# Forgetting attention: one product of 129 columns for two, and a longer read-out at the end of a chunk

## The chip, the cores and the metric

One core of a Trainium2 chip. It has five engines that work side by side, each through its own queue in order: TensorE (PE in the profile, its weight loads PEld), VectorE (DVE), ScalarE (ACT), GpSimd (POOL) and SyncE (SP), which here issues DMAs. TensorE multiplies; its results land in PSUM, the accumulators, eight banks of 512 float32 columns in 128 partitions, from where VectorE and ScalarE read them. Everything else lies in SBUF. The metric is the device time of one execution in microseconds; lower is better. The kernel before takes 1131.02 us, the median of three runs (1130.87 to 1131.43).

## The reference

One decoder layer with two kinds of attention heads beside each other, sequence 2048, width 1024, all float32:

```python
h = rms_norm(x, g_pre) * (1.0 + scale) + shift          # scale, shift, gate from c @ w_ada
qa, ka, va, fa, za, qb, kb, vb, zb = split(h @ w_in)
oa = forgetting_attention(qa, ka, va, fa + b_fgate)      # 8 heads of 64, causal
oa = oa * silu(za)
ob = sliding_window_sink_attention(rope(qb), rope(kb), vb, sinks)   # 8 heads, window 128
y = concatenate([oa, ob * silu(zb)]) @ w_out
return x + gate * rms_norm(y, g_post)

def forgetting_attention(q, k, v, f_logit):              # per head
    cum = cumsum(log_sigmoid(f_logit))
    s = q @ k.T * scale + cum[query] - cum[key]          # -inf above the diagonal
    return softmax(s) @ v
```

The change touches the last line, `softmax(s) @ v`, of the eight forgetting heads.

## The kernel before

float32 values are carried as pairs of float16 numbers, a high and a low part. A product of two such numbers takes three matmuls: high by high, high by low, low by high.

The program goes through stages: normalisation and modulation; the projections; the sliding-window heads, with projections between; the forgetting heads, with the remaining projections and the first of the output products between (some 456 to 977 us); the output projection. In the forgetting stage the order of the work on all engines is written out by hand. A head has four chunks of 512 queries (ci = 0 to 3), and a chunk with index ci has 2 (ci + 1) steps of two key blocks of 128: 20 steps a head (NS), 160 in all. For a step:

- `scores()` (L1414 to L1417) puts the transposed scores of 1024 columns or fewer into one tile `sta` of PSUM (one buffer, two banks);
- `exp32()` (L1421), on ScalarE, takes the exponential into SBUF;
- `high()` (L1425), on ScalarE, makes the high part of the probabilities, `low()` (L1428), on VectorE, the low part, into `pha`;
- `pv()` (L1430 to L1451) multiplies probabilities and values. The probabilities are the stationary operand (a weight load for each matmul), and the values, as they lie in `vt`, are streamed: 129 columns for a key block and a head (VW), of which 0 to 63 are the high part, column 64 is ones (it sums the probabilities, the softmax denominator), 65 to 128 are the low part. For each of up to four query blocks u there are three matmuls: L1438 (65 columns, high by high), L1440 (64 columns, high by low) and L1441 (65 columns, low by high). All add into `poa`, four query blocks of 65 columns, in one bank with a single buffer, over all steps of the chunk.

At the chunk's last step the result is read out: VectorE takes the reciprocal of the four sums (L1445) and multiplies (L1447) into `ona`, which is stored (`o_store`).

The loop over steps (L1749 to L1820) runs, for step s: `exp32` of s; one `tick()`; `low` of s - 1; the first half of the fillers; `high` of s; `scores` of s + 1; a second `tick()`; `pv` of s - 2 (PV_LAG); the second half of the fillers. Fillers are projection matmuls (L361), whose results ScalarE and VectorE take out of PSUM, and matmuls for the row maxima of the next head (L1365), which VectorE reduces (L1368, or with the mask L1370), and at the end of a group of four query blocks turns into rows (L1377 to L1385). `after(n, f)` puts f off to the n-th tick from here. So what `pv` issues directly stands on VectorE ahead of the evacuations of the step's second half; what is put off by one tick stands behind them, in the next step, behind `exp32` of that step on ScalarE and ahead of `low` on VectorE.

Of the kernel before, what the change touches and what calls it, by code (L numbers as in the profile page):

```python
# [10 lines left out]
F32 = mybir.dt.float32  # L11
# [4 lines left out]
AF = mybir.ActivationFunctionType  # L16
ALU = mybir.AluOpType
AX = mybir.AxisListType

P = 128  # L20
# [4 lines left out]
CH = 512  # L25
# [10 lines left out]
XM, XR, VW = 66, 69, 129  # L36
# [7 lines left out]
def hybrid_layer(  # L44
# [17 lines left out]
    V, A, G, PE, SP = nc.vector, nc.scalar, nc.gpsimd, nc.tensor, nc.sync  # L62
# [20 lines left out]
    def sm(n, tag):  # L83
        return small.tile([P, n], F32, tag=tag, name=tag)
# [117 lines left out]
    def after(n, f):  # L202
        late.append([n, f])
# [91 lines left out]
    def o_store(on, pool, ci, rows_, cols_, eng, lag):  # L295
        if ci == 0:
            eng.dma_start(o_d[0][rows_, cols_].rearrange("(u p) c -> p u c", p=P), on)
            return
        u0, u1 = rows_.start // P, rows_.stop // P
        oh = pool.tile([P, u1 - u0, 2, on.shape[-1]], F16, tag="oh", name="oh")  # L300

        def low():
            V.tensor_tensor(oh[:, :, 1], on, oh[:, :, 0], op=ALU.subtract)
            eng.dma_start(o_d[ci][u0:u1, :, :, cols_].rearrange("u n p c -> p (u n) c"),
                          oh[:].rearrange("p u n c -> p (u n) c"))

        after(lag, lambda: A.activation(oh[:, :, 0], on, AF.Copy))
        after(lag + 1, low)
# [174 lines left out]
    start = ExitStack()  # L483
# [298 lines left out]
    def swa_pool(name, bufs, **kw):  # L782
        return swa.enter_context(tc.tile_pool(name=name, bufs=bufs, reuse_waits="tile", **kw))

    op_ = swa_pool("op", 3)
# [146 lines left out]
    class Pair:  # L932
# [65 lines left out]
        def pv(self):  # L998
            j, i = self.j, self.i
            po = ps_pv.tile([P, 4, 64], F32, tag="pv", name="pob")  # L1000
            for e, (i_, k0, nk) in enumerate(self.blocks):
                for h in range(2):
                    for b in range(nk):
                        for n, (pp_, vv) in enumerate(((0, 0), (0, 1), (1, 0))):
                            PE.matmul(po[:, 2 * e + h, :], self.ptt[b + 2 - nk][:, pp_, 2 * e + h, :],  # L1005
                                      vb[:, k0 + b, self.g, 64 * vv:64 * vv + 64],
                                      start=(b == 0 and n == 0), stop=(b == nk - 1 and n == 2))

            def out_():
                on = onp.tile([P, 2, P], F32, tag="on", name="on")  # L1010
                V.tensor_tensor(on[:].rearrange("p e (h d) -> p (e h) d", h=2), po[:],
                                self.rinv[:].unsqueeze(2).broadcast_to([P, 4, 64]), op=ALU.mult)
                o_store(on[:], onp, i // 4, slice((i % 4) * P, (i % 4 + 2) * P), slice((4 + j) * P, (5 + j) * P), G, 1)

            after(1, out_)
# [254 lines left out]
    def fox_pool(name, bufs, **kw):  # L1270
        return fox.enter_context(tc.tile_pool(name=name, bufs=bufs, reuse_waits="tile", **kw))

    ps_st = fox_pool("ps_st", 1, space=PSUM)
    ps_po = fox_pool("ps_po", 1, space=PSUM)
# [4 lines left out]
    op_ = foxl.enter_context(tc.tile_pool(name="opa", bufs=2, reuse_waits="tile"))  # L1279
# [52 lines left out]
    vt, lk, lq = fx["vt"], fx["lk"], fx["lq"]  # L1332
# [63 lines left out]
    class Step:  # L1396
# [33 lines left out]
        def pv(self):  # L1430
            hd, ph = self.hd, self.ph
            if self.first:
                self.po_[0] = ps_po.tile([P, 4, 65], F32, tag="po", name="poa")
            po = self.po_[0]
            for n, (b, u0, o) in enumerate(self.blocks):
                for u in range(u0, 4):
                    pq = slice(o + (u - u0) * P, o + (u - u0 + 1) * P)
                    PE.matmul(po[:, u, :], ph[:, 0, pq], vt[:, b, hd, 0:65],  # L1438
                              start=(self.first and n == 0 and u == 0), stop=False)
                    PE.matmul(po[:, u, 0:64], ph[:, 0, pq], vt[:, b, hd, 65:VW], start=False, stop=False)  # L1440
                    PE.matmul(po[:, u, :], ph[:, 1, pq], vt[:, b, hd, 0:65], start=False,  # L1441
                              stop=(self.last and n == len(self.blocks) - 1))
            if self.last:
                rinv = sm(4, "a_ri")
                V.reciprocal(rinv[:], po[:, :, 64])  # L1445
                on = op_.tile([P, 4, 64], F32, tag="ona", name="ona")
                V.tensor_tensor(on[:], po[:, :, 0:64], rinv[:].unsqueeze(2).broadcast_to([P, 4, 64]), op=ALU.mult)  # L1447
                if hd == 7 and self.ci == 0:
                    for t in range(2):
                        G.tensor_copy(outs[t].o[:, 7 * 64:8 * 64], on[:, t, :])  # L1450
                o_store(on[:], op_, self.ci, slice(0, CH), slice(hd * 64, (hd + 1) * 64), SP, 1 if hd == 7 else 2)  # L1451

        po_ = {}

# [231 lines left out]
    outs = [Out(t) for t in range(NB)]  # L1686
# [26 lines left out]
    with tc.manual_schedule():  # L1713
# [35 lines left out]
        for s, stp_ in enumerate(steps):  # L1749
            hd, r = divmod(s, NS)  # L1750
# [118 lines left out]
```

## Time and profile before

| | before |
|---|---|
| median of three runs | 1131.02 us |
| profiled execution | 1129.92 us, of it span 1128.2 us |
| TensorE busy | 1110.6 us (98%) |
| VectorE busy | 905.6 us (80%) |
| ScalarE busy | 656.8 us (58%) |
| GpSimd busy | 224.6 us (20%) |
| granted TensorE clock | 0.999 |

In the profile's rows `L1438` is a line of the kernel's text. A row of instructions in order of time begins with its start in us from the start of the span and its duration; `[0.29 <-PE poa L1441]` tells how long the engine stood idle before it and what released it. A row of a group ends with busy time, the mean duration in ns, and the idle time before. Ends of matmuls are modelled: a matmul of 65 columns is shown with some 0.19 us, though the next one starts 0.03 us later. What one costs in a stream is therefore read from start to start.

### The profile page before, as it was taken

The numbers are of one execution on the slowest core, as the hardware profiler recorded it, in microseconds if no ns is written. First come the engines' busy times: TensorE is split into PE (matmuls) and PEld (weight loads), VectorE is DVE, ScalarE is ACT, GpSimd is POOL, SyncE is SP. The second block draws the span as 40 slices with busy tenths as digits, with TensorE's granted clock in tenths as the row PEclk, the third lists the DMA queues.
The fourth block names the chain that finished last, engine by engine and source line by source line (L and its number), as shares of the span: only waits on it lengthen the run. The fifth ranks groups of instructions, "written<-read, shape, count | busy, mean of one in ns | idle before, by whom it ended". The sixth has DMA issues, their size and how long they took to land.

```text
span 1128.2 us, 25138 instructions
## 1 busy us (share of the span) xinstructions
PE 1110.6 (98%) x9854; PEld 652.4 (58%) x9854; DVE 905.6 (80%) x1988; ACT 656.8 (58%) x1145; POOL 224.6 (20%) x343
## 2 busy tenths in 40 slices
PE   7899999999999999999999999999999999999997
PEld 2566555676756856556555555655556565544444
DVE  8897488878887468898998989988897997766663
ACT  3974345555555412666766667676666889543332
POOL 3111145545556420010010111001000000100000
PEclk9999999999999999999999999999999999999999
DMA  9854434413333142244223333224311245797632
GB/s 364 280 154 96 81 103 90 93 53 92 83 80 89 39 93 51 65 103 44 58 72 74 86 57 87 51 52 71 72 39 46 76 142 164 153 258 213 193 127 102
DMA packets 124653, 119.77 MB, mean 106 GB/s; under 512 B 66009, under 2 KB 102274, under 8 KB 124534
## 3 DMA queue, kind: packets, MB, share of 16 engines
q1 hardware_dynamic: 113662, 85.66, 28.4%
q0 software_dynamic: 10720, 32.46, 12.6%
q8 instruction: 77, 1.26, 0.6%
q14 instruction: 42, 0.34, 0.1%
q10 hardware_dynamic: 152, 0.04, 0.0%
HBM read 64.43 MB, written 25.18 MB: 79 GB/s over the span
## 4 chain that ended last, share of the span: by engine, by line
PE 83%; DVE 9%; DMA 3%; ACT 3%; issue 2%; SPq 0%; POOL 0%; DVEq 0%; POOLq 0%; ACTq 0%
PE bk L361 32%; PE bk L1650 14%; PE bk L379 7%; PE sta L1414 5%; PE sta L1415 5%; PE bk L1365 5%; PE poa L1440 3%; PE poa L1441 3%; PE poa L1438 3%; PE bk L854 2%; DMA wa<-in_w_ada_dram 2%; PE pss L948 2%; PE pob L1005 1%; PE px L453 1%; DMA xt<-in_x_dram 1%
## 5 line engine op out<-in xcount | busy, mean ns | idle before, releaser
L1421 ACT ACTIVATE p<-sta,lift,scl_qk 128x1024 f32<-128x1024 f32 (+2 forms) x160 | 171.8, 1074 | 128.1 <-PE sta L1415 78.9
L361 PE MATMUL bk<-hT,wh_qk 128*128 128x512 f16 x768 | 196.4, 378 | 0.0
L1428 DVE TENSOR_TENSOR pha<-p,pha 128x1024 f16<-128x1024 f32 (+2 forms) x160 | 168.9, 1056 | 0.2 <-ACT pha L1425 0.2
L1650 PE MATMUL bk<-wohl,oz 128*128 128x512 f16 x744 | 163.2, 379 | 0.0
L1368 DVE TENSOR_REDUCE a_m<-bk 128x1 f32<-128x512 f32 x192 | 130.1, 685 | 37.8 <-PE bk L1365 37.3
L1425 ACT ACTIVATE pha<-p 128x1024 f16<-128x1024 f32 (+2 forms) x160 | 147.8, 924 | 4.9 <-PE poa L1441 0.2
L1650 PEld LDWEIGHTS <-oz 128*128 128x128 f16 x744 | 71.0, 98 | 83.1
L1441 PE MATMUL poa<-vt,pha 128*128 128x65 f16 x1088 | 115.9, 192 | 0.7 <-DVE pha L1428 0.7
L1440 PE MATMUL poa<-vt,pha 128*128 128x64 f16 x1088 | 116.2, 194 | 0.0
L1438 PE MATMUL poa<-vt,pha 128*128 128x65 f16 x1088 | 116.2, 193 | 0.0
L361 PEld LDWEIGHTS <-wh_qk 128*128 128x128 f16 x768 | 71.8, 97 | 73.2 <-issue 1.3
L1414 PE MATMUL sta<-T 128*128 128x512 f16 (+1 forms) x320 | 110.9, 346 | 0.7 <-ACT p L1421 0.7
L1365 PE MATMUL bk<-T 66*128 66x512 f16 (+2 forms) x320 | 110.4, 348 | 0.5 <-DVE a_m L1368 0.2
L1415 PE MATMUL sta<-T 69*128 69x512 f16 (+1 forms) x320 | 109.8, 348 | 0.0
L1438 PEld LDWEIGHTS <-pha 128*128 128x128 f16 x1088 | 101.5, 96 | 14.3 <-issue 0.6
L1440 PEld LDWEIGHTS <-pha 128*128 128x128 f16 x1088 | 100.8, 97 | 11.4
L1441 PEld LDWEIGHTS <-pha 128*128 128x128 f16 x1088 | 100.9, 99 | 0.8 <-DVE pha L1428 0.8
L361 PE MATMUL bk<-hT,wh_za 128*128 128x512 f16 x384 | 100.4, 378 | 0.0
L361 PE MATMUL bk<-hT,wh_zb 128*128 128x512 f16 x384 | 92.1, 379 | 0.0
L379 PE MATMUL bk<-wh_va,hT 128*128 128x256 f16 x768 | 91.9, 273 | 0.0
L361 PE MATMUL bk<-hT,wh_qb 128*128 128x512 f16 x384 | 91.2, 379 | 0.0
L404 POOL DMA_DIRECT2D z_d<-tz x32 | 17.7, 555 | 342.5 <-DVE tz L402 250.9
(463 smaller groups left out, 1956.0 us busy)
## 6 DMA issues: line engine op xcount, KB each, us to landing
hT<-in_x_dram SPq DMA_DIRECT2D x20, 512.0 KB
wa<-in_w_ada_dram SPq DMA_DIRECT2D x16, 512.0 KB
z_d<-tz POOLq DMA_DIRECT2D x32, 256.0 KB, 3.1
T<-z_d SPq DMA_DIRECT2D x16, 512.0 KB
T<-stq SPq DMA_DIRECT2D x60, 128.0 KB
out_dram<-hT SPq DMA_DIRECT2D x15, 512.0 KB
xt<-in_x_dram SPq DMA_DIRECT2D x12, 512.0 KB
qs<-qf SPq DMA_DIRECT2D x80, 64.0 KB
```

The source lines that it names most:

```text
L361: PE.matmul(ps, whl[:, a, k, :], hT[ci][:, b, k, :], start=(k == 0 and n == 0), stop=(k == KT - 1 and n == 2))
L379: PE.matmul(ps[:, (u % 2) * 2 * P:(u % 2 + 1) * 2 * P], hT[ci][:, a, k, u * P:(u + 1) * P], wv[p][:, b, k, :], start=(k == 0 and n == 0), ...
L1365: PE.matmul(mx[:, :w], T[0:XM, 0, i * P:(i + 1) * P], T[0:XM, 2, pc * CH:pc * CH + w], start=True, stop=True)
L1414: PE.matmul(self.st[:, o:o + w], T[:, 3, kb_], T[:, 1, qc], start=True, stop=False)
L1415: PE.matmul(self.st[:, o:o + w], T[0:XR, 2, kb_], T[0:XR, 0, qc], start=False, stop=not diag)
L1421: A.activation(self.p32[:, :self.w], self.st[:, :self.w], AF.Exp, scale=scl[f"qk{self.hd}"][:], bias=lift[:])
L1425: A.activation(self.ph[:, 0, :self.w], self.p32[:, :self.w], AF.Copy)
L1428: V.tensor_tensor(self.ph[:, 1, :self.w], self.p32[:, :self.w], self.ph[:, 0, :self.w], op=ALU.subtract)
L1438: PE.matmul(po[:, u, :], ph[:, 0, pq], vt[:, b, hd, 0:65], start=(self.first and n == 0 and u == 0), stop=False)
L1440: PE.matmul(po[:, u, 0:64], ph[:, 0, pq], vt[:, b, hd, 65:VW], start=False, stop=False)
L1441: PE.matmul(po[:, u, :], ph[:, 1, pq], vt[:, b, hd, 0:65], start=False, stop=(self.last and n == len(self.blocks) - 1))
L1650: PE.matmul(py, self.hl[:, i, k, :], w_slot(8 * j + k)[:, cc], start=(k == 0 and m_ == 0), stop=(k == KT - 1 and m_ == 2))
```

## The change

For the query blocks u = 0, 1, 2 the accumulator has 129 columns in place of 65, so that one matmul streams all of `vt`'s 129 columns past the high probabilities: high by high, the sums, and high by low, in columns of their own. The third matmul (65 columns, low by high) stays as it is. The fourth block keeps its three matmuls, since four times 129 columns don't fit in one bank of 512 (three times 129 and 65 is 452). High by low now lies 65 columns beside the rest and has to be added when the chunk is read out: ScalarE copies those three halves of 64 columns (192 in all) into `ona`, VectorE takes the reciprocals, multiplies the fourth block, adds the three blocks' main halves from PSUM to the copy, and multiplies them. This read-out moves to a function of its own, `out_`, which is put off by one tick.

```diff
             if self.first:
-                self.po_[0] = ps_po.tile([P, 4, 65], F32, tag="po", name="poa")
+                self.po_[0] = ps_po.tile([P, CH], F32, tag="po", name="poa")
...
                     pq = slice(o + (u - u0) * P, o + (u - u0 + 1) * P)
-                    PE.matmul(po[:, u, :], ph[:, 0, pq], vt[:, b, hd, 0:65],
+                    c0, wide = u * VW, VW if u < 3 else 65
+                    PE.matmul(po[:, c0:c0 + wide], ph[:, 0, pq], vt[:, b, hd, 0:wide],
                               start=(self.first and n == 0 and u == 0), stop=False)
-                    PE.matmul(po[:, u, 0:64], ph[:, 0, pq], vt[:, b, hd, 65:VW], start=False, stop=False)
-                    PE.matmul(po[:, u, :], ph[:, 1, pq], vt[:, b, hd, 0:65], start=False,
+                    if u == 3:
+                        PE.matmul(po[:, c0:c0 + 64], ph[:, 0, pq], vt[:, b, hd, 65:VW], start=False, stop=False)
+                    PE.matmul(po[:, c0:c0 + 65], ph[:, 1, pq], vt[:, b, hd, 0:65], start=False,
                               stop=(self.last and n == len(self.blocks) - 1))
             if self.last:
-                rinv = sm(4, "a_ri")
-                V.reciprocal(rinv[:], po[:, :, 64])
-                on = op_.tile([P, 4, 64], F32, tag="ona", name="ona")
-                V.tensor_tensor(on[:], po[:, :, 0:64], rinv[:].unsqueeze(2).broadcast_to([P, 4, 64]), op=ALU.mult)
...
+                after(1, self.out_)
+
+        def out_(self):
+            hd, po = self.hd, self.po_[0]
+            on = op_.tile([P, 4, 64], F32, tag="ona", name="ona")
+            p3 = po[:, 0:3 * VW].rearrange("p (u c) -> p u c", c=VW)
+            A.activation(on[:, 0:3], p3[:, :, 65:VW], AF.Copy)
+            rinv = sm(4, "a_ri")
+            V.reciprocal(rinv[:], po[:, 64:3 * VW + 65:VW])
+            V.tensor_scalar(on[:, 3], po[:, 3 * VW:3 * VW + 64], rinv[:, 3:4], None, op0=ALU.mult)
+            V.tensor_tensor(on[:, 0:3], on[:, 0:3], p3[:, :, 0:64], op=ALU.add)
+            V.tensor_tensor(on[:, 0:3], on[:, 0:3], rinv[:, 0:3].unsqueeze(2).broadcast_to([P, 3, 64]), op=ALU.mult)
...
+            o_store(on[:], op_, self.ci, slice(0, CH), slice(hd * 64, (hd + 1) * 64), SP, 1 if hd == 7 else 2)
```

In the changed text the products are L1439 (129 columns, or 65 for the fourth block), L1442 (64) and L1443 (65), the copy is L1452, and VectorE's four operations are L1454 to L1457.

How the instructions stand, at the end of the first chunk (head 0, ci = 0). VectorE before (`a_ri` are the reciprocals, `lq` the limbs of the next head's row maxima, `pha` the probabilities):

```order
L1368 TENSOR_REDUCE a_m<-bk_5995 128x1 [waits PE_49]
L1445 RECIPROCAL a_ri<-poa 128x4 [waits PE_49]
L1447 TENSOR_TENSOR ona<-poa,a_ri 128x256 [waits DVE_49]
L1368 TENSOR_REDUCE a_m<-bk_139 128x1 [waits PE_49]
L1370 ISA bk_137,a_m<-bk_137,cmask 128x512 [waits PE_49]
L1370 ISA a_m 128x1
L1377 TENSOR_REDUCE a_m_6651<-a_m 128x4 [waits DVE_49]
L1382 TENSOR_SCALAR lq_1661<-a_m_6651 128x4 [waits DVE_49]
L1384 SCALAR_TENSOR_TENSOR a_mr<-lq_1661,a_m_6651 128x4 [waits DVE_49]
L1385 TENSOR_SCALAR lq_1661<-a_mr 128x4 [waits DVE_49]
```

and now:

```order
L1368 TENSOR_REDUCE a_m<-bk_139 128x1 [waits PE_49]
L1370 ISA bk_137,a_m<-bk_137,cmask 128x512 [waits PE_49]
L1370 ISA a_m 128x1
L1377 TENSOR_REDUCE a_m_6640<-a_m 128x4 [waits DVE_49]
L1382 TENSOR_SCALAR lq_1661<-a_m_6640 128x4 [waits DVE_49]
L1384 SCALAR_TENSOR_TENSOR a_mr<-lq_1661,a_m_6640 128x4 [waits DVE_49]
L1385 TENSOR_SCALAR lq_1661<-a_mr 128x4 [waits DVE_49]
L1454 RECIPROCAL a_ri<-poa 128x4 [waits Activation_49]
L1455 TENSOR_SCALAR ona<-poa,a_ri 128x64 [waits DVE_49]
L1456 TENSOR_TENSOR ona<-ona,poa 128x192
L1457 TENSOR_TENSOR ona<-ona,a_ri 128x192 [waits DVE_49]
L1428 TENSOR_TENSOR pha<-p_6598,pha 128x1024
```

The read-out moved from ahead of seven operations (a maximum, a masked maximum with its second half, and four on the rows) to behind them, and its first operation now waits for ScalarE. TensorE, at the first product of the next chunk, before (`identb` and `dmaskT` are the mask's matmul of the scores):

```order
L1417 MATMUL sta<-dmaskT,identb 128x128
L1438 LDWEIGHTS pha [waits DVE_49]
L1438 MATMUL poa<-vt,pha 128x65 [waits PE_49]
L1440 LDWEIGHTS pha
L1440 MATMUL poa<-vt,pha 128x64
L1441 LDWEIGHTS pha
L1441 MATMUL poa<-vt,pha 128x65
```

and now:

```order
L1417 MATMUL sta<-dmaskT,identb 128x128
L1439 LDWEIGHTS pha [waits DVE_49]
L1439 MATMUL poa<-vt,pha 128x129 [waits Activation_49]
L1443 LDWEIGHTS pha
L1443 MATMUL poa<-vt,pha 128x65
```

The first weight load waited for VectorE's last reading of `poa` before and does so now; the matmul behind it now also waits for ScalarE's copy.

More of the change, by code (lines that the diff above doesn't have):

```diff
@@ L1442, in pv @@
+                    PE.matmul(po[:, c0:c0 + 65], ph[:, 1, pq], vt[:, b, hd, 0:65], start=False,
                               stop=(self.last and n == len(self.blocks) - 1))
             if self.last:
-                rinv = sm(4, "a_ri")
-                V.reciprocal(rinv[:], po[:, :, 64])
-                on = op_.tile([P, 4, 64], F32, tag="ona", name="ona")
[L1447 to L1450, printed above, removed]
@@ L1451, in pv @@
-                o_store(on[:], op_, self.ci, slice(0, CH), slice(hd * 64, (hd + 1) * 64), SP, 1 if hd == 7 else 2)
+                after(1, self.out_)
[9 more added lines that the diff above has]
+            V.tensor_tensor(on[:, 0:3], on[:, 0:3], rinv[:, 0:3].unsqueeze(2).broadcast_to([P, 3, 64]), op=ALU.mult)
+            if hd == 7 and self.ci == 0:
+                for t in range(2):
+                    G.tensor_copy(outs[t].o[:, 7 * 64:8 * 64], on[:, t, :])
+            o_store(on[:], op_, self.ci, slice(0, CH), slice(hd * 64, (hd + 1) * 64), SP, 1 if hd == 7 else 2)
```

## The prediction

> **What bounds the kernel now.** I read the page's head first, then TensorE's own waits in the forgetting-attention stage (440 to 985 us), then that stage in windows.
>
> ```profile
> span 1128.2 us, 25138 instructions
> ```
>
> ```profile
> PE sta L1414 <- ACT p L1421: 0.7, 3, 0.3
> PE poa L1441 <- DVE pha L1428: 0.7, 1, 0.7
> PE bk L1365 <- DVE a_m L1368: 0.2, 1, 0.2
> ```
>
> ```profile
> 456.00:980.00 524.00, 522.59 (x5470) 305.94 (x5469) 461.58 (x996) 375.27 (x461) 39.03 (x62) 1.00 0.34 77
> 880.00:924.00 44.00, 43.03 (x512) 26.41 (x509) 42.90 (x85) 37.71 (x49) 0.54 (x1) 1.00 0.41 112
> ```
>
> The three wait rows are all that TensorE waited between 440 and 985 us: 1.6 us. The windows (columns: length, then busy time of TensorE, weight loads, VectorE, ScalarE, GpSimd) say the same: TensorE 522.59 of 524. So each nanosecond taken from its queue counts there, and each new wait of it counts too, since almost nothing stands in the schedule that could absorb it. VectorE is busy 461.58 of 524, with its queue nearly full from 880 to 924. That is room on average; whether it is in the right place is the question below.
>
> **What the products save.** Per key block and query block there are three products; 1088 of each kind stand in the row below. For three of four query blocks in a full chunk, and 768 in all (1088 less 8 heads x 40 blocks with u = 3), two of 65 and 64 columns become one of 129. Prices are taken from start to start, since ends are modelled.
>
> ```profile
> 609.30 0.19 PE L1438 MATMUL poa<-vt,pha 128*128 128x65 f16 x1
> ...
> 610.04 0.22 PE L1322 MATMUL bk<-identh,lq 128*72 128x128 f16 x1
> ```
>
> ```profile
> L1438 PE MATMUL poa<-vt,pha x1088: 191/193/205, 456.2 to 976.3; 128*128 128x65 f16 x182
> ```
>
> ```profile
> L854 PEld LDWEIGHTS <-hT x384: 95/98/100, 46.2 to 121.4; 128*128 128x128 f16 x192
> ```
>
> ```profile
> 86.15 5.68 PE bk L854 x96
> ...
> 382.99 6.55 PE bk L379 x60
> ```
>
> From 609.30 to 610.04 run 24 products: 0.74/24 = 30.8 ns each, 92.5 per triple. With a weight load for every product, 136 columns (L854) take 5.68/96 = 59.2 ns and 256 columns (L379) 6.55/60 = 109.2. That is 0.417 ns a column, so 129 columns take 56.3. A triple becomes 56.3 + 30.8 = 87.1: 5.4 ns less, times 768 = **4.1 us**. Bounds: at least 92.5 - 59.2 - 30.8 = 2.5 ns (1.9 us), if 129 columns cost as much as 136; at most 7 ns (5.4 us), if the product after a wide one also loses the 1.6 ns by which 30.8 exceeds the line through the two rows at 65 columns (29.6, an estimate). The columns streamed stay the same; only one instruction's overhead goes.
>
> **What the read-out costs.** At the end of each of 32 chunks (8 heads x 4) ScalarE gets a copy of 192 columns, and VectorE four operations in place of two.
>
> ```profile
> L1445 DVE RECIPROCAL a_ri<-poa 128x4 f32<-128x4 f32 x32 | 5.7, 177 | 4.7 <-PE poa L1441 4.6
> L1447 DVE TENSOR_TENSOR ona<-poa,a_ri 128x256 f32<-128x256 f32 x32 | 13.6, 424 | 1.2
> L1382 DVE TENSOR_SCALAR lq<-a_m 128x4 f16<-128x4 f32 x32 | 5.4, 170 | 1.1
> L866 DVE SCALAR_TENSOR_TENSOR vb<-bk,vb 128x128 f16<-128x128 f32 x16 | 3.9, 284 | 1.3 <-ACT vb L862 1.3
> L862 ACT ACTIVATE vb<-bk 128x128 f16<-128x128 f32 x16 | 3.5, 274 | 9.4 <-PE bk L854 9.4
> L1147 ACT ACTIVATE stq<-bk 128x512 f16<-128x512 f32 x30 | 17.8, 592 | 31.1 <-PE bk L361 30.4 <-DMA T<-rw 0.7
> ```
>
> Copy of 192: between 274 and 592, on the line through them 0.33 us. The sum and the product of 192 columns: between 284 and 424, 0.35 each. The 64 columns alone: between 170 and 284, 0.22, of which the next instruction overlaps some. With the reciprocal first, from the point at which VectorE comes to the read-out to the end of the sum, which is the last reading of the accumulator, it is 0.22 + 0.18 + 0.36 = **0.76 us**. All four take some 0.5 us more of VectorE than the two before: 16 us over the stage, inside its 62 idle us, so as load it is costed at nothing; were that room taken already, it would cost up to 16.
>
> What matters is the place. There is one accumulator (one bank, one buffer): the first product of the next chunk waits for the last reading. Before, the two operations stood directly behind the last product of the chunk. Now they are issued at the next tick, behind the evacuations of the step's second half, and behind the copy, which stands behind the next exponential on ScalarE; in the changed order the reciprocal waits for ScalarE, and the first product's weight load for VectorE. Queued behind that load is everything on TensorE. So at each chunk end the question is whether VectorE gets there before TensorE does. A typical end of a chunk ci = 0 (VectorE, TensorE, ScalarE):
>
> ```profile
> 527.07 0.18 DVE L1445 RECIPROCAL a_ri<-poa 128x4 f32<-128x4 f32 x1
> 527.28 0.42 DVE L1447 TENSOR_TENSOR ona<-poa,a_ri 128x256 f32<-128x256 f32 x1
> 527.63 0.68 DVE L1368 TENSOR_REDUCE a_m<-bk 128x1 f32<-128x512 f32 x1
> 528.22 0.69 DVE L1370 CUSTOM_DVE_ANT_0 bk<-bk,cmask 128x512 f32<-128x512 f32 x1
> ...
> 529.69 1.22 DVE L1428 TENSOR_TENSOR pha<-p,pha 128x1024 f16<-128x1024 f32 x1
> ```
>
> ```profile
> 526.59 0.19 PE L1438 MATMUL poa<-vt,pha 128*128 128x65 f16 x1
> ...
> 527.73 0.38 PE L1365 MATMUL bk<-T 66*128 66x512 f16 x1
> ...
> 529.11 0.19 PE L1438 MATMUL poa<-vt,pha 128*128 128x65 f16 x1
> ```
>
> ```profile
> 526.79 1.10 ACT L1421 ACTIVATE p<-sta,lift,scl_qk 128x896 f32<-128x896 f32 x1 [0.85 <-PE sta L1417]
> ```
>
> Before, the reading ended at 527.70, and TensorE came at 529.11: 1.4 us of room. Now seven operations stand ahead of it. Taking out 0.6 us in front of them helps little: the 512-wide maximum (528.22) needs the product of 527.73, which ends at 528.11. VectorE is through them at about 529.6, the sum ends at 529.7 + 0.76 - 0.1 = 530.4, and TensorE, ready at 529.1, stands for **1.3 us**. ScalarE's copy (from 527.9, ended by 528.3) is not the late one here. As a rule: wait = start of the L1428 behind the group, + 0.76, - start of the next chunk's first L1438. First and last of the eight ci = 0 ends:
>
> ```profile
> 463.16 1.22 DVE L1428 TENSOR_TENSOR pha<-p,pha 128x1024 f16<-128x1024 f32 x1
> ...
> 925.85 1.22 DVE L1428 TENSOR_TENSOR pha<-p,pha 128x1024 f16<-128x1024 f32 x1
> ```
>
> ```profile
> 462.59 0.19 PE L1438 MATMUL poa<-vt,pha 128*128 128x65 f16 x1
> ...
> 923.93 0.20 PE L1438 MATMUL poa<-vt,pha 128*128 128x65 f16 x1
> ```
>
> They give 1.3 and 2.7 us. The eight ci = 0 ends sum to 12.2 by this rule, the ci = 1 and ci = 2 ends (most have few operations in the group and no wait) to about 4. At ci = 3 ends there is one operation in the group and the copy decides:
>
> ```profile
> 520.05 1.20 ACT L1421 ACTIVATE p<-sta,lift,scl_qk 128x1024 f32<-128x1024 f32 x1 [2.02 <-PE sta L1415]
> ```
>
> ```profile
> 522.68 0.19 PE L1438 MATMUL poa<-vt,pha 128*128 128x65 f16 x1
> ```
>
> Exponential to 521.25, copy to 521.6, sum to 522.4: 0.3 us early. Two ends of this kind, with TensorE sooner, miss by 0.3: 0.6 us. Together **17 us of new waits**, with 10.6 if every group moves up by the full 0.6 us that is taken out ahead of it, and 19 + 1.5 if the copy is 0.5 us dearer than on the line and five ci = 3 ends miss too.
>
> The Trainium skill speaks against having both engines at this bank ("PSUM — Partial Sum Buffer", PSUM bank collisions raise a hardware error): two engines must not touch one bank of the same partitions at once, readers included. By that the copy and VectorE's readings can only follow each other, as the changed order has it; no run here shows a collision.
>
> **The sum.** Profiled execution 1129.9 us (span 1128.2 plus 1.7 around it); + 17 - 4.1, and - 0.5 of the 1.6 us that TensorE waits now, which a late TensorE no longer waits: 1142.3. The median shown is 1131.0, 1.1 above that execution: **1143 us**. Low: 10.6 - 5.4 - 1.6 = +3.6, 1135. High: 20.5 - 1.9 = +18.6, 1150.
>
> **Rivals.** (a) *Faster.* The order hides the read-out: VectorE arrives at the read-out before TensorE at every end, as it does now with 1.4 us of room, and only the 4.1 us are left: 1127. It decides below 4.1 us of waits in all, 0.5 us per ci = 0 end. For it: most ci = 1 to ci = 3 ends have the room. Against: the chain 527.73, maximum, four small operations, read-out cannot be shortened by a faster queue, and it stands in each head.
> (b) *No change.* Waits near 4 us, under half the low bound, with the saving at its middle: 1131. For it only the many small terms that I cost from neighbouring shapes.
> (c) *Much slower.* VectorE's load becomes the bound: every one of 31 ends stands for 1.3 us, 40 in all, less 4: 1167. For it the stretch 880 to 924 (42.90 of 44). Against it 461.58 of 524 over the stage; the waits themselves give VectorE time to catch up.
> (d) *Dear wide products.* The wide product would stand for its own weight load, 98 ns in the L854 row, in place of 56.3, where the pair costs 61.6 now: 768 x 36.4 = +28 in place of -4.1, so 1175. Against it that same L854: a weight load each, and 59.2 from start to start. The Trainium skill ("TensorE: Matmul & The Clock Gate", Back-to-back issue gap) speaks for a milder form: some 81 ns per product at 128 columns in streams of loads and products, by which the term would be +15 and the time 1162; the trace disagrees with it at 136 columns.
> That the change doesn't do what it says I exclude: TensorE's order falls from 19216 to 17680 rows, 2 x 768.
>
> **How the numbers follow.** Forecast 0.83, (a) 0.04, (b) 0.04, (c) 0.07, (d) 0.02. The likeliest gives 1143; 1135 to 1150 covers its own bounds and leaves out (c), (d) and (a), 0.13, and a little of its own tails. Faster by over 0.2% (2.3 us, about what a measurement can tell from none): 0.04; within: 0.04; slower: 0.92.
>
> **What would show it.** In the changed profile TensorE's waits should have a new first row, the first product at L1439 waiting for VectorE's sum (L1456), some 12 to 20 times, 10 to 20 us in total, the longest 2 to 3 us in head 7, ci = 0 ends over 1 us. TensorE's busy share in 456 to 990 falls by 3 points. Triples start 87 ns apart. I am wrong if that row is under 4 us, if the products cost otherwise, or if the time stands in another wait: banks (L1365 or L361 behind VectorE) or exponentials (L1414 behind ScalarE).

## The result and the profile after

The changed kernel takes **1150.4 us** (median of 4 runs, 1149.7 to 1151.7), the kernel before 1131.2 on the same chip: a ratio of 1.0169 (95% interval 1.0156 to 1.0181). Forecast were 1143 us and a range up to 1150. The direction and the place are as forecast, the size is not: +19.2 us where +12 stood.

The head of the page, and the rows of TensorE's waits in the forgetting stage (440 to 1000 us, which now ends 22 us later):

```profile
span 1150.0 us, 23695 instructions
```

```profile
PE poa L1439 <- DVE ona L1456: 15.0, 12, 2.7
PE bk L1365 <- DVE wohl L1521: 2.8, 2, 1.4
PE poa L1439 <- ACT p L1421: 1.3, 1, 1.3
PE sta L1414 <- ACT p L1421: 0.3, 1, 0.3
PE bk L1365 <- DVE a_m L1368: 0.2, 1, 0.2
```

Before, three rows summed to 1.6 us. Now the first product of a chunk (L1439) stands 13 times, 16.3 us, for the end of the read-out. In the third row (at 568.07 us) the releaser named is an exponential that ended at 568.03, 0.03 us behind the accumulator's sum (L1456, 567.66 and 0.34 long). The product reads nothing of that exponential, and its weight load is shown as waiting 1.77 us for L1456, so the row belongs to the first. The second row is a wait that the prediction did not speak of; it is read below, and it isn't VectorE's either.

The windows of this stage and of its last part, beside those shown of before (524.00 us with TensorE busy 522.59):

```profile
456.00:1000.00 544.00, 524.46 (x4698) 303.24 (x4697) 475.92 (x1057) 378.13 (x492) 39.14 (x61) 0.99 0.33 74
880.00:924.00 44.00, 39.95 (x380) 23.39 (x379) 40.18 (x96) 33.94 (x44) 0.00 (x0) 1.00 0.29 72
```

TensorE's busy time is 1.9 us more than before, and the window is 20 us longer: nearly all of the added time is idle time of TensorE. Its clock reads 0.99 in place of 1.00, which matters below. One end of a chunk as the trace shows it (head 4, ci = 0):

```profile
738.48 0.70 DVE L1370 CUSTOM_DVE_ANT_0 bk<-bk,cmask 128x512 f32<-128x512 f32 x1 [0.17 <-PE bk L1365]
...
739.38 0.22 PE L1417 MATMUL sta<-dmaskT,identb 128*128 128x128 bf16 x1
...
740.08 0.69 DVE L1140 SCALAR_TENSOR_TENSOR stq<-bk,stq 128x512 f16<-128x512 f32 x1
740.69 0.17 DVE L1454 RECIPROCAL a_ri<-poa 128x4 f32<-128x4 f32 x1
740.90 0.28 DVE L1455 TENSOR_SCALAR ona<-poa,a_ri 128x64 f32<-128x64 f32 x1
741.10 0.34 DVE L1456 TENSOR_TENSOR ona<-ona,poa 128x192 f32<-128x192 f32 x1
741.48 0.36 DVE L1457 TENSOR_TENSOR ona<-ona,a_ri 128x192 f32<-128x192 f32 x1
741.50 0.10 PEld L1439 LDWEIGHTS <-pha 128*128 128x128 f16 x1 [2.07 <-DVE ona L1456]
```

TensorE has issued all it has by 739.4. VectorE is still in the group of evacuations of that step, comes to the read-out at 740.69, and its last reading of the accumulator ends at 741.44, 0.75 us later (forecast 0.76). TensorE's weight load stands for 2.07 us. L1457, behind it, reads the accumulator no more and holds nobody.

### The profile page after: what moved, and what is told of

Its sections match the earlier page's. It is cut to its first block, busy times and chain, and to the rows that moved or that the text cites. A ratio compares the mean times of both kernels' runs of the same rounds, so it can differ in the third digit from the quotient of the medians.

```text
span 1150.0 us, 23695 instructions
## 1 busy us (share of the span) xinstructions
PE 1114.7 (97%) x9086; PEld 650.5 (57%) x9086; DVE 922.0 (80%) x2052; ACT 660.2 (57%) x1177; POOL 224.8 (20%) x343
## 4 chain that ended last, share of the span: by engine, by line
PE 76%; DVE 15%; ACT 4%; issue 3%; DMA 2%; POOL 0%; DVEq 0%; POOLq 0%; ACTq 0%
PE bk L361 29%; PE bk L1660 13%; PE bk L379 7%; PE bk L1365 4%; PE poa L1439 4%; PE sta L1415 4%; PE sta L1414 4%; PE poa L1443 2%; PE bk L854 2%; PE pss L948 1%; PE pob L1005 1%; DVE a_m L1368 1%; DVE pha L1428 1%; ACT p L1421 1%; PE px L453 1%
## 5 line engine op out<-in xcount | busy, mean ns | idle before, releaser
L1425 ACT ACTIVATE pha<-p 128x1024 f16<-128x1024 f32 (+2 forms) x160 | 147.8, 923 | 14.2 <-PE poa L1443 11.7
L1439 PE MATMUL poa<-vt,pha 128*128 128x129 f16 (+1 forms) x1088 | 113.3, 213 | 16.3 <-DVE ona L1456 15.0
L1439 PEld LDWEIGHTS <-pha 128*128 128x128 f16 x1088 | 98.9, 97 | 35.0 <-DVE ona L1456 22.5
L1443 PE MATMUL poa<-vt,pha 128*128 128x65 f16 x1088 | 113.8, 193 | 0.0
L1414 PE MATMUL sta<-T 128*128 128x512 f16 (+1 forms) x320 | 111.1, 347 | 0.3 <-ACT p L1421 0.3
L1443 PEld LDWEIGHTS <-pha 128*128 128x128 f16 x1088 | 96.8, 98 | 10.2
L379 PEld LDWEIGHTS <-hT 128*128 128x128 f16 x768 | 73.4, 98 | 12.1 <-issue 2.1
L1370 DVE CUSTOM_DVE_ANT_0 bk<-bk,cmask 128x128 f32<-128x128 f32 (+3 forms) x128 | 63.1, 495 | 15.1 <-PE bk L1365 15.0
```

What stands on the lines that cost most here:

```text
L379: PE.matmul(ps[:, (u % 2) * 2 * P:(u % 2 + 1) * 2 * P], hT[ci][:, a, k, u * P:(u + 1) * P], wv[p][:, b, k, :], start=(k == 0 and n == 0), ...
L1414: PE.matmul(self.st[:, o:o + w], T[:, 3, kb_], T[:, 1, qc], start=True, stop=False)
L1425: A.activation(self.ph[:, 0, :self.w], self.p32[:, :self.w], AF.Copy)
L1439: PE.matmul(po[:, c0:c0 + wide], ph[:, 0, pq], vt[:, b, hd, 0:wide], start=(self.first and n == 0 and u == 0), stop=False)
L1443: PE.matmul(po[:, c0:c0 + 65], ph[:, 1, pq], vt[:, b, hd, 0:65], start=False, stop=(self.last and n == len(self.blocks) - 1))
```

## The experiments

Ratios are to the kernel before, timed beside it on the same chip.

### Is it the place, or the products?

First, the changed kernel with the read-out put back to where it stood:

```diff
-                after(1, self.out_)
+                self.out_()
```

> The changed kernel with one edit: the read-out is issued directly behind the chunk's last product, not put off by one tick. Theory 'place' (the new waits come from where the read-out stands on VectorE, behind the evacuations of the step's second half): TensorE's waits at the next chunk's first product fall from some 19 us to under 4, and the time to 1129 to 1133 us. Theory 'operations' (the copy on ScalarE, the engines' exclusion at the bank and the longer read-out make the wait, wherever they stand): 10 us or more of waits stay, 1142 or more.

Measured: 1132.2 us, ratio 1.0013 (1.0003 to 1.0022). The rows of L1439 are gone:

```profile
PE sta L1414 <- ACT p L1421: 2.9, 8, 0.5
PE poa L1443 <- DVE pha L1428: 1.2, 2, 0.9
PE bk L1365 <- DVE a_m L1370: 0.6, 1, 0.6
```

The one tick makes some 18 of the 19 us. The other half of the pair: the kernel before, products and both read-out operations as they were, with the read-out one tick later (no copy, no sum).

```diff
             if self.last:
-                rinv = sm(4, "a_ri")
-                V.reciprocal(rinv[:], po[:, :, 64])
...
+                after(1, self.out_)
+
+        def out_(self):
+            rinv = sm(4, "a_ri")
+            V.reciprocal(rinv[:], po[:, :, 64])
```

> The kernel before with one edit: products and read-out operations as they were (two operations on VectorE), but put off by one tick. Theory 'place': the same waits at the first product of the chunks behind a ci = 0 end, each some 0.2 us shorter, and the waits of the key stores: 1143 to 1148 us. Theory 'operations': within 3 us of before, 1131 to 1134.

Measured: 1151.0 us, ratio 1.0177 (1.0160 to 1.0194), more than expected. Its waits:

```profile
PE poa L1438 <- DVE ona L1451: 12.5, 11, 2.3
PE bk L1365 <- DMA T<-sv: 3.2, 2, 2.1
```

The place alone slows the kernel as much as the whole change does. By starts its first products wait 14.8 us, and 18.8 in the changed kernel, whose read-out is longer: that longer read-out takes back what the products save. The second row, here with the releaser's right name, is TensorE waiting for stored keys, a term that this expectation named and the prediction did not have. The trace has a third term, which neither had: 6.8 us at half clock from 902.55 us on, read below.

The products alone: read-out in its old place, three VectorE operations, and the high-by-low part of three query blocks left out of the sum (so this kernel leaves out a part of the computation, and is a bound, not a version).

```diff
-            A.activation(on[:, 0:3], p3[:, :, 65:VW], AF.Copy)
...
-            V.tensor_tensor(on[:, 0:3], on[:, 0:3], p3[:, :, 0:64], op=ALU.add)
-            V.tensor_tensor(on[:, 0:3], on[:, 0:3], rinv[:, 0:3].unsqueeze(2).broadcast_to([P, 3, 64]), op=ALU.mult)
+            V.tensor_tensor(on[:, 0:3], p3[:, :, 0:64], rinv[:, 0:3].unsqueeze(2).broadcast_to([P, 3, 64]), op=ALU.mult)
```

> Wide products with the read-out where it stood before, three operations on VectorE; the halves high by low of three of four query blocks are not added to the result (that sum is left out). It measures what the products alone save. If a triple of 92 ns becomes a pair of 87 as the rows of the changed profile say (57.6 + 29.5): 1127 to 1128.5 us. If a wide product saves nothing: 1131 or, with a longer read-out by one operation, 1132.

Measured: 1128.1 us, ratio 0.9974 (0.9965 to 0.9984). From start to start all products of probabilities and values take 100.06 us before and 96.63 here: 3.4 us saved, of which new small waits (L1443 for the low half, L1414 for the exponential) take some back. In the changed kernel three pairs of a wide and a narrow product fill 0.26 us, 87 ns each:

```profile
615.88 0.22 PE L1439 MATMUL poa<-vt,pha 128*128 128x129 f16 x1
615.94 0.19 PE L1443 MATMUL poa<-vt,pha 128*128 128x65 f16 x1
...
616.14 0.19 PE L1439 MATMUL poa<-vt,pha 128*128 128x65 f16 x1
```

### Which ends cost

The read-out in its old place at the eight ends of ci = 0 alone; the other 24 stay put off.

```diff
-                after(1, self.out_)
+                if self.ci == 0:
+                    self.out_()
+                else:
+                    after(1, self.out_)
```

> The change with the read-out in its old place at the ends of the shortest chunks (ci = 0) alone; the 24 other ends stay put off. By the prediction's table the ends of ci = 0 carry 12.2 of 17 us of waits; in the changed kernel's trace they carried 13.2 of 18.8, with the two longest (2.06 and 2.84 us), behind which TensorE's clock fell to half. Theory: waits of 5 to 6 us stay at the first products, no stretch at half clock, and the time is 1133 to 1138 us (the upper part if the two waits for the stored keys stay as they are, 3.1 us). Rival: every end costs about alike (18.8/31 each), so 14 us of waits stay and the time is 1143 to 1147 us.

Measured: 1138.4 us, ratio 1.0055 (1.0041 to 1.0069). From start to start 5.9 us of waits stay at the first products, 3.1 us at the stored keys, and no stretch runs at half clock. A quarter of the ends carries two thirds of the loss, about as the prediction's sum had it (12.2 of 17 us of waits).

### The wait for stored keys

TensorE's second row names VectorE's L1521. The view of the transfers of stored keys (L1142, from 890 us on) shows, under who waited for them, these same two waits:

```profile
L1142 SPq DMA_DIRECT2D T<-sv x2: 629/647/665, 901.3 to 919.7; - x2
...
  PEld L1365: 3.0, 2
```

The timeline (start, length) of SyncE's queue, VectorE and TensorE around the first of them, of the kernel before:

```profile
883.97 0.40 SPq L304 DMA_DIRECT2D o_d<-oh  x1
884.46 0.67 SPq L1142 DMA_DIRECT2D T<-sv  x1
```

```profile
883.52 0.41 DVE L303 TENSOR_TENSOR oh<-ona,oh 128x256 f16<-128x256 f32 x1
```

```profile
887.44 0.38 PE L1365 MATMUL bk<-T 66*128 66x512 f16 x1
```

And of the changed kernel:

```profile
900.84 0.40 SPq L304 DMA_DIRECT2D o_d<-oh  x1
901.33 0.67 SPq L1142 DMA_DIRECT2D T<-sv  x1
```

```profile
900.39 0.42 DVE L303 TENSOR_TENSOR oh<-ona,oh 128x256 f16<-128x256 f32 x1
```

```profile
902.34 0.19 PE L1443 MATMUL poa<-vt,pha 128*128 128x65 f16 x1
903.84 0.39 PE L1365 MATMUL bk<-T 66*128 66x512 f16 x1 [1.31 <-DVE wohl L1521]
```

The transfer of the next keys (L1142) stands on SyncE's queue behind the store of the attention output (L304), and that waits for its low half (L303), which is issued a fixed number of ticks after the read-out. A read-out one tick later puts L303, the store and the keys one tick later. Against TensorE's own progress that is 1.9 us: TensorE comes to these keys 14.9 us later than before (887.44 there, 902.37 now), the queue to L1142 16.9 us later. Before there were 0.5 us of room. So TensorE stands 1.5 us here, and 1.6 at 920.

Is this a cause of its own? The changed kernel with the store one tick earlier again (heads 0 to 6):

```diff
-            o_store(on[:], op_, self.ci, slice(0, CH), slice(hd * 64, (hd + 1) * 64), SP, 1 if hd == 7 else 2)
+            o_store(on[:], op_, self.ci, slice(0, CH), slice(hd * 64, (hd + 1) * 64), SP, 1)
```

> The changed kernel with one edit: the store of the result is put off by one tick less in heads 0 to 6, so that it is issued in the same tick as in the kernel before. Theory 'queue': in the changed kernel the store of the result stands on SyncE's queue ahead of the store of the next head's keys and, a tick late, holds it up; TensorE then waits for the keys (L1365, twice, 3.1 us in the changed profile). Here these two waits go and the time is 1147 to 1148 us. Theory 'load' (VectorE's full queue between 880 and 924 us makes these waits): they stay, 1150.

Measured: 1151.6 us, ratio 1.0179 (1.0164 to 1.0195). The wait is gone and the time stayed:

```profile
PE poa L1439 <- DVE ona L1456: 15.9, 13, 2.0
PE poa L1443 <- DVE pha L1428: 1.0, 1, 1.0
PE sta L1414 <- ACT p L1421: 0.9, 2, 0.6
PE bk L1365 <- DMA T<-sv: 0.3, 1, 0.3
```

Since that compared two chips, it was run again beside the changed kernel, together with the opposite edit, a late store alone in the kernel before (`1 if hd == 7 else 2` made `2 if hd == 7 else 3`; the ends of ci = 0 store without this delay, so this moves the 24 others).

> The kernel before (products and read-out as they were, in their place), with the attention output stored one tick later at every end: the row of the low half (L303) and the store behind it on SyncE's queue, ahead of the stored keys (L1142). In the kernel before the keys land about 0.5 us before TensorE comes for them, twice, near 887 and 904 us. Theory store: one tick is 1.9 to 3 us, so TensorE waits 1.4 to 2.5 us at L1365 in each of the two places, 3 to 5 us in all, and the time grows by 2 to 5 us: ratio 1.002 to 1.005. Rival: VectorE's full queue between 880 and 924 stops TensorE there anyway (0.7 us at L1441 in the kernel before), so the wait at L1365 takes the place of others: ratio 1.000 to 1.0015.

> The changed kernel itself once more, on the chip on which the two beside it run, to compare them run by run: ratio 1.016 to 1.018 again, first products waiting 18 to 19 us by starts, L1365 waiting 3 us for the stored keys.

> The changed kernel with its store one tick earlier in heads 0 to 6, as once before, beside the changed kernel on the same chip. Theory store: the 3.1 us of waits for stored keys are a term of their own; without them the ratio falls by 0.002 to 0.003, to 1.013 to 1.015. Rival load: VectorE's queue stops TensorE next in the same stretch, and the ratio is the changed kernel's within 0.001.

Measured: the late store alone 1134.1 us, ratio 1.0029 (1.0018 to 1.0041); the changed kernel 1151.1, ratio 1.0177 (1.0164 to 1.0191); the changed kernel with the earlier store 1149.9, ratio 1.0171 (1.0157 to 1.0185). Alone, the late store costs 3.3 us, by waits of 2.0 and 1.2 us (by starts) and by what stood behind the first, below. Who waited for L1142 there:

```profile
L1142 SPq DMA_DIRECT2D T<-sv x2: 624/644/665, 887.3 to 907.4; - x2
...
  PEld L1365: 3.1, 2
```

In the changed kernel taking it out returns 1.1 us between medians, which lies inside both intervals. So each theory's range holds in one kernel: alone, the late store is a cause, and in the changed kernel, with it away, other waits of the same stretch (VectorE's low half at L1443, 1.0 us, the exponential, 0.9) come forward.

### TensorE at half clock behind long waits

Behind the two longest waits the windows of the changed kernel show a lower clock (last but two column):

```profile
742.00:746.00 4.00, 4.00 (x21) 1.67 (x19) 2.67 (x6) 0.52 (x1) 0.00 (x0) 0.57 0.59 166
746.00:750.00 4.00, 4.00 (x47) 2.49 (x46) 2.21 (x8) 2.63 (x3) 0.00 (x0) 1.00 0.34 97
940.00:944.00 4.00, 1.33 (x18) 1.00 (x17) 3.79 (x14) 2.35 (x5) 0.07 (x1) 0.96 0.64 164
944.00:948.00 4.00, 4.00 (x27) 2.87 (x25) 2.63 (x4) 1.13 (x2) 1.68 (x2) 0.61 0.35 98
```

Cut at the right places, such a stretch reads 0.50 and is 3.41 us long:

```profile
738.88:742.29 3.41, 1.51 (x27) 1.26 (x26) 3.17 (x12) 1.07 (x2) 0.15 (x1) 1.00 0.87 24
742.29:745.70 3.41, 3.41 (x12) 1.24 (x9) 2.38 (x6) 0.52 (x1) 0.00 (x0) 0.50 0.61 173
```

Products of 512 columns start 0.43 us apart there, not 0.22:

```profile
744.90 0.63 PE L1414 MATMUL sta<-T 128*128 128x512 f16 x1
745.33 0.57 PE L1415 MATMUL sta<-T 69*128 69x512 f16 x1
```

To see which wait does that, a staircase: the kernel before, with more and more VectorE work ahead of the read-out at two ends of each head (425 ns for each operation in the trace; `dum` is a tile of its own, 256 columns).

```diff
             if self.last:
+                if self.ci in (1, 2):
+                    for _ in range(3 + 2 * hd):
+                        V.tensor_tensor(dum[:], dum[:], dum[:], op=ALU.mult)
                 rinv = sm(4, "a_ri")
```

> The kernel before, with added VectorE work ahead of the read-out at the ends of ci = 1 and ci = 2: 3 operations on 128x256 in head 0, two more in each later head, 17 in head 7 (some 0.35 us each by neighbouring rows, so 1 to 6 us). The first product of the next chunk then waits 0 to about 4.5 us, once in each step of this staircase and twice per head. Theory length: behind a wait of up to 1.9 us the products of 512 columns go on at some 215 ns from start to start, behind one of 2.8 us or more at some 427 ns for 3 to 6 us, at whatever place of the stage it stands; where between 2.0 and 2.8 it begins is what the staircase tells. Rival place: the half clock in the changed kernel belonged to those two stretches (739 to 745 and 941 to 948 us) and the waits in other places leave the clock at 1.00. Rival sum: what counts is idle time gathered over tens of microseconds; then single waits of 2 to 3 us in a stretch that is otherwise full leave the clock alone, and it falls only in the last heads.

Measured: 1196.5 us (one run). Idle time of TensorE by starts, and what its products took beyond full clock behind it:

| wait, us | 0.89 | 0.95 | 1.67 | 1.94 | 2.13 | 2.45 | 2.85 | 2.88 | 3.89 | 4.70 | 5.20 | 5.40 | 7.18 |
|---|---|---|---|---|---|---|---|---|---|---|---|---|---|
| lost behind it, us | 0 | 0 | 0 | 1.7 | 1.7 | 1.7 | 1.7 | 1.7 | 1.7 | 2.4 | 2.8 | 2.5 | 2.5 |

Windows behind the wait of 1.94 us, with and behind that of 1.67, and behind that of 5.20:

```profile
568.50:572.50 4.00, 4.00 (x28) 1.75 (x25) 4.00 (x7) 2.17 (x3) 2.03 (x3) 0.57 0.23 31
709.00:713.00 4.00, 2.50 (x33) 1.35 (x32) 3.86 (x11) 1.75 (x3) 0.00 (x0) 1.00 0.00 0
713.00:717.00 4.00, 3.64 (x38) 2.06 (x37) 3.96 (x7) 2.01 (x2) 2.13 (x4) 1.00 0.20 71
...
922.50:927.50 5.00, 5.00 (x23) 2.19 (x21) 4.50 (x10) 2.22 (x3) 0.00 (x0) 0.52 0.14 22
```

Theory length holds in this run, with an onset below 2 us. Behind each wait of 1.94 to 3.89 us one stretch of 3.41 us runs at half clock and 1.7 us are lost; behind the four waits from 4.70 us on the clock falls before TensorE goes on, for 6.8 or 10.2 us, and 2.4 to 2.8 us are lost. The place does not matter, and no gathering of idle time over tens of microseconds is needed.

The other traces show that length alone does not decide. Behind the same end of head 4 (2.06 us of waiting) one execution of the changed kernel fell to half clock (span 1150.0 us) and another did not (1148.0). In the kernel with the place alone changed, TensorE stood 2.50 us until 944.9, longer than in four of the falls above, and the clock stayed:

```profile
940.10:943.51 3.41, 2.50 (x26) 1.47 (x23) 3.41 (x7) 3.41 (x5) 0.54 (x1) 1.00 0.28 90
943.51:946.92 3.41, 1.98 (x33) 1.68 (x34) 2.99 (x9) 1.57 (x3) 1.75 (x2) 1.00 0.66 154
```

The stretches at half clock of one execution start whole multiples of 3.41 us apart (742.29 and 943.68: 59 times), so they lie on a grid, and between two executions of the changed kernel this grid lies 1.06 us differently against the program. Counting TensorE's idle time in each step of the grid sorts the waits of the traces that have such stretches: every step with 2.06 us or more idle is followed by one at half clock, no step at full clock with 1.87 or less is, and of six steps between 1.91 and 2.02 four are. The wait of 2.50 us lay across two steps, 1.1 and 1.4 us. That was read from the traces; no run moved a wait against the grid. Why the clock stayed at half for two steps behind a wait of 2.31 us in the kernel with the place alone changed (6.8 us from 902.55 on) stays open.

The late store alone paid it too: behind its wait of 1.96 us 1.7 us went at half clock, in an execution that took 1135.2 us, 4.4 more than the kernel before.

### Can the saving be kept?

The direct read-out costs about what it saves (1.0013 against 0.9974 for the products alone). Where? Variants of it:

VectorE's copy:

```diff
-            A.activation(on[:, 0:3], p3[:, :, 65:VW], AF.Copy)
+            V.tensor_copy(on[:, 0:3], p3[:, :, 65:VW])
```

> The change with its read-out directly behind the last product, as in the direct variant (1132.19 us), but the halves of the three blocks are copied by VectorE and not by ScalarE. Theory ScalarE: what the direct variant lost against the products alone (1132.19 to 1128.06) is ScalarE's copy, which waits for the last product of the chunk and holds up the next exponential; its rows were the scores waiting for the exponential (2.9 us in 8 waits) and the products waiting for the low half (1.2 us). With the copy on VectorE the first of these rows falls below 1 us, and the time is 1128.0 to 1129.5 us. Rival load: the two added VectorE operations (0.32 + 0.34 us at each of 32 ends) are what costs; the low halves come later still, the wait at L1443 grows above 3 us, and the time is 1131 to 1134 us.

The same, with the ends of ci = 3 put off (and copied by ScalarE):

```diff
-                self.out_()
+                if self.ci == 3:
+                    after(1, self.out_)
+                else:
+                    self.out_()
```

> The change with the read-out put off (copy by ScalarE) at the ends of the longest chunks (ci = 3) alone; at the others it stands directly behind the last product, with the copy on VectorE. By the prediction's reading the ends of ci = 3 have one operation in the group ahead of the read-out and cost 0.6 us together when they are put off: the first product waits 0 to 1 us for VectorE's sum in all, and the time stands within 1 us of the variant that is direct everywhere with VectorE's copy (1128 to 1130 us). Rival: every put-off end costs, whatever stands in its group, some 0.6 us each: the time is 1133 to 1136 us.

ScalarE copies all, GpSimd multiplies:

```diff
             A.activation(on[:, 0:3], p3[:, :, 65:VW], AF.Copy)
+            A.activation(on[:, 3], po[:, 3 * VW:3 * VW + 64], AF.Copy)
...
-            V.tensor_scalar(on[:, 3], po[:, 3 * VW:3 * VW + 64], rinv[:, 3:4], None, op0=ALU.mult)
             V.tensor_tensor(on[:, 0:3], on[:, 0:3], p3[:, :, 0:64], op=ALU.add)
-            V.tensor_tensor(on[:, 0:3], on[:, 0:3], rinv[:, 0:3].unsqueeze(2).broadcast_to([P, 3, 64]), op=ALU.mult)
+            G.tensor_tensor(on[:], on[:], rinv[:].unsqueeze(2).broadcast_to([P, 4, 64]), op=ALU.mult)
```

> The wide products with the read-out directly behind the last product; ScalarE copies the second halves of three blocks (192 columns) and the fourth block (64), VectorE takes the reciprocal and the sum alone (177 + 344 ns, less than the 177 + 424 of the kernel before), and the last multiplication (256 columns) goes to GpSimd, which is busy 39 of 524 us. Theory load: the direct variants lost their 3 to 4 us against the products alone because VectorE had 0.5 to 0.8 us more to do at each of 32 ends; with VectorE's part back at its old length the loss goes, and the ratio to the kernel before is 0.997 to 0.999. Rival hold-up: what costs is that ScalarE's copies (now two) wait for the last product ahead of the next exponential; then the scores wait 3 us or more for the exponential, and the ratio is 1.000 to 1.003.

And two in which only the three blocks' multiplication goes to GpSimd (`G.tensor_tensor` in place of the last `V.tensor_tensor`), with ScalarE's copy and with VectorE's:

> As the direct variant with ScalarE's copy, but the last multiplication of the three blocks (192 columns) is done by GpSimd. VectorE keeps reciprocal, fourth block and sum: 0.2 us more than the kernel before at an end in place of 0.56. Theory load: half or more of the loss of the direct variant (1.0013) against the products alone (0.9974) comes back, ratio 0.998 to 1.000. Rival hold-up: ScalarE's copy ahead of the exponential is what costs, and the ratio stays 1.000 to 1.002.

> As the direct variant with VectorE's copy (1.0011), but the last multiplication of the three blocks is done by GpSimd: VectorE has 0.5 us more than the kernel before at an end in place of 0.85. Theory load: the ratio falls by about 0.001 to 0.002, to 0.999 to 1.000. Rival hold-up: ScalarE's copy was what cost in its sister; here it isn't there, so the ratio falls below 0.999.

Measured:

| variant (read-out in the old place) | ratio, 95% interval | TensorE waits more than in the kernel before, by starts |
|---|---|---|
| products alone (sum left out) | 0.9974 (0.9965 to 0.9984) | 1.4 us |
| ScalarE's copy | 1.0013 (1.0003 to 1.0022) | 4.9 |
| VectorE's copy | 1.0011 (1.0002 to 1.0020) | 4.8 |
| VectorE's copy, ends of ci = 3 put off | 1.0017 (1.0008 to 1.0026) | 5.1 |
| ScalarE copies all, GpSimd multiplies | 1.0017 (1.0008 to 1.0025) | 4.2 |
| ScalarE's copy, GpSimd multiplies | 1.0006 (0.9998 to 1.0015) | 4.0 |
| VectorE's copy, GpSimd multiplies | 1.0005 (0.9996 to 1.0014) | 3.3 |

None beats the kernel before. With ScalarE's copies the scores wait for an exponential that stands behind a copy that waits for the chunk's last product. The row in the variant where ScalarE copies all:

```profile
PE sta L1414 <- ACT p L1421: 3.8, 7, 0.8
```

In the variant with VectorE's copy that row is 1.2 us, and the first product waits 0.8:

```profile
PE sta L1414 <- ACT p L1421: 1.2, 3, 0.7
PE poa L1443 <- DVE pha L1428: 1.2, 2, 1.0
PE poa L1439 <- DVE ona L1456: 0.8, 1, 0.8
```

So in the variant with VectorE's copy the ratio (1.0011) fits the rival load, but neither theory's sign is there: the scores still wait 1.2 us where less than 1 was expected without ScalarE's copy, and L1443 waits 1.2 us where the load was to make it over 3. Where ScalarE copies all, ratio and row are those of the rival hold-up. With GpSimd's multiplication of the three blocks the ratio is the hold-up's with ScalarE's copy (1.0006) and neither's with VectorE's (1.0005). The variants wait 3 to 5 us more than the kernel before, about the 3.4 us that the products save, whichever engine takes the added read of 192 columns. The ends of ci = 3 put off gave 1.3 us of waits by starts, against 0 to 1 expected; that ratio can't be told from its neighbours'. How the rest splits between load and order isn't settled.

## Why the prediction fell short

By the steps of its sum:

| step | forecast, us | measured, us |
|---|---|---|
| products | -4.1 (bounds -5.4 to -1.9) | -3.4 |
| waits of the first product for the read-out | +17 (10.6 to 20.5) | +18.8 by starts, 16 times |
| waits for stored keys behind the attention output's store | not named | +3.1 |
| TensorE at half clock behind its waits of 2.06 and 2.84 us | not named | about +3.4 in this execution (1.7 behind each) |
| other waits: of before that fall away, less small new ones | -0.5 | -1.2 |

The measured rows sum to +20.7. In the trace the stage grew by 21.0: its first and last scores start at 446.3 and 970.9 us before, at 447.2 and 992.8 after. The profiled execution (1151.7 us) is the longest of the four; another one of the same program (1149.8) had one of the two stretches at half clock. The terms that the forecast named come to +14.2, with which it would have been 1145; the two that it did not name make up the rest.

- **Right: the main mechanism.** The one accumulator, the read-out behind the group of evacuations at the next tick, the first product's weight load waiting for the sum. It forecast L1439 waiting for L1456, 12 to 20 times, 10 to 20 us, the longest 2 to 3 us in head 7; the page has 13 waits, 16.3 us and 2.7, and by starts the longest, 2.84 us, is head 7's. The ends of ci = 0 carry 13.2 us (forecast 12.2). The read-out's 0.76 us was 0.75; its parts were off in both directions (L1455 284 ns, forecast 0.22; L1452 322, forecast 0.33). The experiments on the place show the cause.
- **Right in kind, mis-sized by 0.7 us: the products.** 87 ns for a wide and a narrow product, as worked out from the line of 0.417 ns a column, and 3.4 us over all. Rival (d), the dear wide product at 98 ns, falls: 57 ns from start to start. So does the milder form by the Trainium skill ("TensorE: Matmul & The Clock Gate", Back-to-back issue gap), some 81 ns at 128 columns; this stream has a weight load for every product.
- **Wrong: that the move's cost is all at the first product.** The step "what matters is the place" followed one tensor, the accumulator. The read-out's other product, `ona`, goes on through ScalarE, L303 and a store on SyncE's queue, and those were moved too: 24 of the 32 ends store by that chain, and twice the next keys stand behind it. The step was to count every queue past which the read-out moves, and SyncE's was left out. Its price alone is 3.3 us; in the changed kernel TensorE stands 3.1 us for it, but taking it out returned no more than 1.1, which is not clear of the noise.
- **Wrong: that a wait costs its own length.** The high end of the range summed waits only. Waits of 2.06 and 2.84 us were each followed by 3.41 us at half clock, which cost 1.7 us more. The profile of before could not show it, since its longest wait in this stage is 0.7 us.
- **VectorE's added load, costed at nothing (up to 16 us).** As load at the new place it is in the first product's wait, which the sum has: 18.8 us with the four operations, 14.8 with the two old ones. With the read-out in its old place it does not hide either: copy and sum bring 2 to 4 us of waits more than the products alone.
- **Rivals.** (a) and (b) fall; (c), every end waiting 1.3 us, falls too: 16 of 31 wait.

So the step that failed is the one from the place to the price: it charged the move with the first product's wait alone. The two terms that it left out, of the same sign as the main one, carried the time just past the range's end; that the end was missed by so little is chance, since the time moves by a microsecond or two with how often the clock falls.

## What to carry to other kernels

Before putting an operation off, follow everything that hangs on its output to the last queue, and look for what stands behind those DMAs on it; the operation's own reader is only the first that comes late. A saving on the engine that bounds the kernel counts only if what replaces it finds room on the others at that place: here 3.4 us of TensorE's time were spent again on an added read of the accumulator, on whichever engine. And an engine that must stay full is best charged more than the wait for a stop of some 2 us or longer: here 1.7 us on top, in those executions in which the clock fell.

## What the runs showed of the hardware

TensorE's granted clock falls to half (0.50 over 742.29 to 745.70 us) for 3.41 us behind a stop of about 2 us, beginning within 1.5 us of its resuming, and this cost 1.7 us; once, behind 2.31 us, it was 6.8 us. Behind stops of 4.7 to 7.2 us it was 6.8 or 10.2 us, in part within the stop, and cost 2.4 to 2.8 us. In this stage of these runs stops up to 1.86 us left the clock alone and those from 2.83 us on never did. Between 1.92 and 2.50 us both occurred, at 2.06 in two executions of one program; how much of the stop lay in one step of a grid of 3.41 us sorts nearly all of them, with the border at 1.9 to 2.0 us of a step. The Trainium skill ("TensorE: Matmul & The Clock Gate", Part 1: The HAM clock gate) tells of a gate that goes to half after an idle window of about 3.4 us, in windows that run free of the program. The length of the stretches, the grid, which lay differently in two executions, and the doubled spacing (0.43 us at 512 columns) agree with that. That the window must be idle does not: 2.06 us of one were enough.
